# Opening of a two-layer mixer trunk: c and x loaded first, scale and shift rows divided between VectorE and TensorE, rotary tables made inside the group loop

## The chip, the cores and the metric

One core of one Trainium2 chip runs the whole program. The metric is the device time of one execution in microseconds (us), the median of several runs. TensorE (PE) does matmuls and transposes, VectorE (DVE) and ScalarE (ACT) the elementwise work, SyncE (SP) issues every DMA. The program's text is a list of calls; a scheduler gives each engine a fixed order ahead of time, and each engine then runs its own list strictly in that order, held only by semaphores.

## The reference

The kernel computes a trunk of two layers on 256 tokens of width 2048. What this change touches is the head of each layer:

```python
c_act = jax.nn.silu(c)
cos_r, sin_r = rope_tables(positions, RET_DK)
cos_m, sin_m = rope_tables(positions, MLA_ROPE)
...
mod = c_act @ w_mod + b_mod
shift, scale, gate = jnp.split(mod, 3, axis=-1)
h = rms_norm(x, g_norm) * (1.0 + scale[:, None, :]) + shift[:, None, :]
proj = h @ w_in
```

`h` then feeds a retention branch and a latent attention branch, which are gated, merged and projected back. The rotary tables depend on `positions` alone, so they are the same in both layers.

## The kernel before, in words

**Layout.** Activations are kept with features on the partitions: `xT` is 16 blocks of 128 features by 256 tokens. A weight tile is 128 x 1024 f32 (512 KB): SP loads it into `wst` (5 buffers), ACT rounds it to a high part and DVE subtracts to get the low part, both into `whl` (`split_into`, L239 to L241; 3 buffers). A product is three matmuls, high x high, high x low and low x high (`chunk`, L267). One such 512 KB tile is called a chunk below: with 128x256 outputs it is 24 matmuls (16 at L273, 8 at L276), with 128x512 outputs 12.

**The first products.** Before anything else can be multiplied, `h` must exist, and `h` needs 4096 values of scale and shift, each a sum over 2048 rows of `w_mod`. So layer 0 works in four groups of four feature blocks (`GROUPS`, L49). `first_products` (L595) runs 14 columns of `w_in` for one group while the scale and shift rows of the next group are formed in the background: `mod_pair` (L404) loads 16 tiles into `ring` (2 buffers) and DVE adds them, weighted by `cact`, into `macc`. `mod_finish` splits the sum into bf16 pieces, 12 small matmuls with a vector of ones add it over the partitions (`mod_sum`, L351), and DVE puts the result into `mods` (L357) and `amul` (L426). Then DVE normalises a pair of blocks (L446), ACT applies scale and shift (L454) and rounds to `h` high, and DVE makes `h` low (L241). Layer 1 has two groups of eight blocks.

**The opening.** Group 0 has nothing to hide behind, so `start` (L508) writes PE, DVE and ACT's order by hand (`manual_schedule`): the tiles of `w_mod` for group 0 are eight for the scale (`ws[1, k]`) and eight for the shift (`ws[0, k]`), each with two of the 16 row blocks `k`. PE forms the scale row from all 16 (L542, with `cact` as weights); DVE forms the shift row from all 16 (L347, L349), which is summed over the partitions by four matmuls (`mod_sum` at L554). `vectors(0)` (L175) loads `b_mod`, norm gains and `c` as 88 rows and turns them with one transpose. x comes in four 512 KB tiles, is squared by ACT, turned by 32 transposes (L532) and copied to `xT` by ACT (L534). The rotary tables (`rotary_tables`, L215: ten DVE operations on 128x512 or 128x256, then four ACT operations) are made once, in the opening, and read by the rope steps later.

```python
for k0 in range(0, KT - nd, nd):
    mod_rows(acc, ws[0, k0], k0, nd)
A.activation(row[0:1, :], pr[0:1, : ng * P], AF.Copy)
mod_sum(0, 16, ng, [row[0:1, :]], ones[0:1, 0:1])
make_amul(0, 0, ng)
mod_rows(acc, ws[0, KT - nd], KT - nd, nd)
for k in range(ng):
    V.tensor_scalar(xh0[:, k, :], xh0[:, k, :], amul[0][:, k : k + 1], None, ALU.mult)
prepared.append(load_split(first[0], 2, 512, early=True))
mod_sum(0, 0, ng, [acc], ones[:, 0:1])
```

Of the kernel before, what the change touches and what calls it, by code (L numbers as in the profile page):

```python
# [108 lines left out]
def trunk(ctx: ExitStack, tc: tile.TileContext, x, c, positions, w_mod, b_mod, g_norm, w_in, g_cq,  # L109
# [63 lines left out]
    vec = [cp.tile([P, 72 if l else 88], F32, name=f"vec{l}") for l in range(DEPTH)]  # L173

    def vectors(l):  # L175
        rows = tp.tile([P, P], F32, name="rows", tag="tmp")
# [7 lines left out]
        ps = aux_tile()
        T.transpose(ps[:, :r0], rows[:r0, :], ident[:r0, :r0])
        V.tensor_copy(vec[l][:, :r0], ps[:, :r0])

    vectors(0)
# [4 lines left out]
    cact = cp.tile([P, KT], F32, name="cact")  # L193
    A.activation(cact, vec[0][:, 72:88], AF.Silu)

    posi = tp.tile([P, S], I32, name="posi", tag="tmp")
    DMA.dma_start(posi, positions.broadcast_to([P, S]))
    pos = dp.tile([P, S], F32, name="pos", tag="dtab")

# [308 lines left out]
    def start():  # L508
# [6 lines left out]
        row, acc = extra[:, : ng * P], extra[:, 512 : 512 + ng * P]  # L515
        xh0, hh = blocks("xh0"), Pairs("h")
        with tc.manual_schedule(engines={ENG.PE, ENG.DVE, ENG.Activation}):
            for q in range(2):
# [2 lines left out]
            rotary = rotary_tables(quarter("angle"))
            next(rotary)
            v = small(2)
            V.tensor_tensor(v, ss[:, 0, :], ss[:, 1, :], ALU.add)
            V.tensor_scalar(v, v, 1.0 / D, EPS, ALU.mult, ALU.add)
            y = rsqrt_small(v, 2)
            for pair in range(KT // 2):
# [12 lines left out]
            for k0 in range(0, KT, nd):  # L540
                for k in range(nd):
                    T.matmul(pr[0:1, : ng * P], cact[:, k0 + k : k0 + k + 1], ws[1, k0][:, k, :], start=k0 + k == 0,  # L542
                             stop=k0 + k == KT - 1)
            for k0 in range(0, KT - nd, nd):
# [3 lines left out]
            make_amul(0, 0, ng)
            mod_rows(acc, ws[0, KT - nd], KT - nd, nd)
            for k in range(ng):  # L550
                V.tensor_scalar(xh0[:, k, :], xh0[:, k, :], amul[0][:, k : k + 1], None, ALU.mult)
# [479 lines left out]
```

## Time and profile before

| | |
|---|---|
| median of 3 runs | 2054.24 us (2052.72 to 2056.39) |
| the profiled execution's own time | 2055.65 us |
| its span in the trace | 2053.9 us |
| PE busy | 2024.4 us (99%) |
| PE weight loads (PEld) busy | 1807.5 us (88%) |
| DVE busy | 1483.3 us (72%) |
| ACT busy | 1061.9 us (52%) |
| HBM traffic | 223 GB/s over the span |

The span is cut into what each engine did. [...] A row of the timeline gives the start in us, the busy time in us, the engine, the source line, output and inputs, how many instructions, and in brackets how long the engine sat idle before it and what ended that. SPq is SP's queue of DMA issues.

### The profile page before, as it was taken

To read this page: it belongs to the slowest core of one execution; us is meant where nothing else is said; L and a number is where in the kernel's file an instruction comes from. 1 tells how busy PE (TensorE), PEld (TensorE's weight loads), DVE (VectorE), ACT (ScalarE), POOL (GpSimd) and SP (SyncE) were. 2 spreads that over 40 slices of the span, in tenths; PEclk is the share of its full clock that TensorE was granted. 3 is DMA by queue.
4 is the path that set the end of the run, shared out by engine and by line. 5 is a ranking of instruction groups with operands and counts; after the bars stand their busy time and mean duration, and the time that the engine had idled before them with its cause. 6 is when DMAs were issued, how large, how long until landed. Compare 5 with 4: busy or idle time off the path is not lost.

```text
span 2053.9 us, 31775 instructions
## 1 busy us (share of the span) xinstructions
PE 2024.4 (99%) x12412; PEld 1807.5 (88%) x12414; DVE 1483.3 (72%) x2082; ACT 1061.9 (52%) x1489; POOL 0.2 (0%) x4
## 2 busy tenths in 40 slices
PE   7999999999999999999999999999999999999998
PEld 4888898998899998889998888889889999988887
DVE  5789996788777777775577775568766877765574
ACT  4554355644456664444454464456544666644453
POOL 0000000000000000000000000000000000000000
PEclk9999999999999999999999999999999999999999
DMA  8988966567866668875569976665677666666672
GB/s 309 336 287 281 310 202 194 156 191 257 309 191 196 194 185 274 284 267 185 183 197 339 317 214 187 194 180 158 196 240 223 203 186 195 210 224 192 190 243 90
DMA packets 251222, 460.59 MB, mean 224 GB/s; under 512 B 18464, under 2 KB 68032, under 8 KB 251072
## 3 DMA queue, kind: packets, MB, share of 16 engines
q1 hardware_dynamic: 251072, 458.57, 69.9%
q8 instruction: 97, 1.59, 0.3%
q14 instruction: 53, 0.43, 0.1%
HBM read 456.41 MB, written 2.10 MB: 223 GB/s over the span
## 4 chain that ended last, share of the span: by engine, by line
PE 96%; DVE 1%; DMA 1%; ACT 1%; issue 0%; SPq 0%; ACTq 0%; DVEq 0%
PE acc L273 58%; PE acc L276 29%; DMA wmod<-in_w_mod 1%; PE aux L264 1%; PE aux L265 1%; PE aux L263 1%; PE acc L263 1%; PE acc L264 1%; PE acc L265 1%; DVE extra L349 0%; PE aux L882 0%; PE aux L723 0%; PE aux L909 0%; PE aux L848 0%; PE aux L849 0%
## 5 line engine op out<-in xcount | busy, mean ns | idle before, releaser
L240 ACT ACTIVATE whl<-wst 128x1024 fp32r<-128x1024 f32 (+1 forms) x708 | 709.1, 1007 | 810.8 <-PE acc L276 703.4
L241 DVE TENSOR_TENSOR whl<-wst,whl 128x1024 fp32r<-128x1024 f32 (+1 forms) x708 | 814.5, 1156 | 386.7 <-ACT whl L240 383.4
L273 PE MATMUL acc<-whl,h 128*128 128x512 f32 x2048 | 512.2, 391 | 0.0
L273 PEld LDWEIGHTS acc<-whl,h 128*128 128x128 f32 x2048 | 382.1, 188 | 78.2
L273 PE MATMUL acc<-h,whl 128*128 128x256 f32 x2432 | 328.6, 286 | 4.0 <-ACT h L240 2.4
L273 PEld LDWEIGHTS acc<-h,whl 128*128 128x128 f32 x2432 | 308.9, 193 | 6.2 <-ACT h L240 3.2
L276 PE MATMUL acc<-whl,h 128*128 128x512 f32 x1024 | 278.5, 391 | 0.0
L273 PE MATMUL acc<-whl,z 128*128 128x512 f32 x1024 | 254.1, 390 | 1.2 <-ACT whl L240 1.2
L273 PEld LDWEIGHTS acc<-whl,z 128*128 128x128 f32 x1024 | 191.9, 188 | 41.3 <-ACT whl L240 1.6
L276 PEld LDWEIGHTS acc<-whl,h 128*128 128x128 f32 x1024 | 191.3, 188 | 39.5 <-DVE whl L241 0.4
L276 PE MATMUL acc<-h,whl 128*128 128x256 f32 x1216 | 177.8, 286 | 0.0
L276 PEld LDWEIGHTS acc<-h,whl 128*128 128x128 f32 x1216 | 160.2, 194 | 0.0
L276 PE MATMUL acc<-whl,z 128*128 128x512 f32 x512 | 137.3, 389 | 0.0
L402 DVE SCALAR_TENSOR_TENSOR macc<-ring,cact,macc 128x1024 f32<-128x1024 f32 x75 | 96.1, 1281 | 32.0 <-DMA ring<-in_w_mod 31.8
L402 DVE SCALAR_TENSOR_TENSOR macc<-wst,cact,macc 128x1024 f32<-128x1024 f32 x90 | 115.0, 1278 | 0.0
L276 PEld LDWEIGHTS acc<-whl,z 128*128 128x128 f32 x512 | 96.0, 188 | 20.1 <-DVE whl L241 0.2
L273 PE MATMUL acc<-c,whl 128*128 128x256 f32 x640 | 101.1, 289 | 0.0
L273 PEld LDWEIGHTS acc<-c,whl 128*128 128x128 f32 x640 | 86.3, 191 | 0.3
L273 PE MATMUL acc<-m,whl 128*128 128x256 f32 x512 | 67.3, 283 | 0.0
L273 PEld LDWEIGHTS acc<-m,whl 128*128 128x128 f32 x512 | 64.0, 192 | 0.1
L276 PE MATMUL acc<-c,whl 128*128 128x256 f32 x320 | 57.9, 285 | 0.0
L273 PE MATMUL acc<-whl,m 128*128 128x512 f32 (+1 forms) x256 | 56.5, 365 | 0.0
(256 smaller groups left out, 1871.8 us busy)
## 6 DMA issues: line engine op xcount, KB each, us to landing
wst<-in_w_in SPq DMA_DIRECT2D x416, 512.0 KB, 4.4
wst<-in_w_mod SPq DMA_DIRECT2D x96, 512.0 KB, 4.7
ring<-in_w_mod SPq DMA_DIRECT2D x80, 512.0 KB, 5.1
wst<-in_w_ret_proj SPq DMA_DIRECT2D x64, 512.0 KB, 4.8
wst<-in_w_mla_proj SPq DMA_DIRECT2D x64, 512.0 KB, 4.2
wst<-in_w_out SPq DMA_DIRECT2D x64, 512.0 KB, 3.7
wst<-in_w_ukv SPq DMA_DIRECT2D x32, 512.0 KB, 4.3
wst<-in_w_uq SPq DMA_DIRECT2D x32, 384.0 KB, 4.1
```

What stands on the lines that cost most here:

```text
L240: A.activation(hi, src, AF.Copy)
L241: return V.tensor_tensor(lo, src, hi.bitcast(F32), ALU.subtract)
L263: T.matmul(o, a[0], b[0], start=start, stop=False, skip_group_check=True)
L264: T.matmul(o, a[0], b[1], start=False, stop=False, skip_group_check=True)
L265: T.matmul(o, a[1], b[0], start=False, stop=stop, skip_group_check=True)
L273: T.matmul(o, x, y, start=start and i == 0, stop=False, skip_group_check=True)
L276: T.matmul(o, x, y, start=False, stop=stop, skip_group_check=True)
L402: V.scalar_tensor_tensor(macc, w, cact[:, k : k + 1], macc, ALU.mult, ALU.add)
```

## The change

- `c` has a load of its own, directly behind the constants, and is turned and passed through SiLU by itself (PE, then ACT). x is loaded next. `b_mod`, the gains and `positions` are loaded behind the eight scale tiles, and turned and converted after the scale row (`turned()`, and the CAST of `pos`).
- The first four pairs of x blocks are copied to `xT` by DVE, the other four by ACT.
- The scale row is divided: row blocks 0 to 5 on DVE (into `macc`), 6 to 15 on PE (L556 of the new file); eight small matmuls add both parts into one PSUM tile (L563, L566).
- The shift row is divided: row blocks 0 to 11 on DVE, 12 to 15 on PE, with the `w_mod` tile itself as weights and a column of `cact` moving (16 matmuls, L579); four matmuls add DVE's part between them (L583).
- `rotary_tables` is taken out of `start`. It is called in `first_products`, in the loop over the groups and outside the `if` above it, so once for each of the four groups of layer 0 and the two of layer 1. `pos` stays alive until the last of them, in one of the two `dtab` buffers that also hold `r`, the decay tables and the squares of layer 0's end.

```diff
+    crow = tp.tile([P, P], F32, name="crow", tag="tmp")
+    DMA.dma_start(crow[:KT, :], c[0].rearrange("(r q) -> r q", q=P))
...
-        ws = {(i, k): mod_fetch(quarter("wmod"), 0, 16 * i, k, ng) for i in (1, 0) for k in range(0, KT, nd)}
+        ws = {(1, k): mod_fetch(quarter("wmod"), 0, 16, k, ng) for k in range(0, KT, nd)}
+        turned = vectors(0)
+        posi = tp.tile([P, S], I32, name="posi", tag="tmp")
+        DMA.dma_start(posi, positions.broadcast_to([P, S]))
+        ws.update({(0, k): mod_fetch(quarter("wmod"), 0, 0, k, ng) for k in range(0, KT, nd)})
...
+            mod_rows(scale, ws[1, 0], 0, nd)
             for k in range(0, ng, 2):
                 normalise(xh0[:, k : k + 2, :], k, r)
-            next(rotary, None)
+            for k0 in range(nd, on_v, nd):
+                mod_rows(scale, ws[1, k0], k0, nd)
             pr = aux_tile()
...
+            turned()
+            V.tensor_copy(pos[0], posi)
...
+            for k0 in range(0, KT - on_t, nd):
                 mod_rows(acc, ws[0, k0], k0, nd)
...
+            for k0 in range(KT - on_t, KT, nd):
+                for k in range(k0, k0 + nd):
+                    for b in range(ng):
+                        T.matmul(ps[:, b : b + 1], ws[0, k0][:, k - k0, b * P : (b + 1) * P], cact[:, k : k + 1],
+                                 start=k == KT - on_t and b == 0, stop=k == KT - 1, skip_group_check=True)
+                if k0 == KT - on_t:
+                    for b in range(ng):
+                        T.matmul(ps[:, b : b + 1], acc[:, b * P : (b + 1) * P], ones[:, 0:1], start=False, stop=False,
+                                 skip_group_check=True)
+            V.tensor_tensor(mods[0][:, 0:ng], ps[:, :ng], bm[0][:, 0:ng], ALU.add)
             first = [w_in[0, k0 * P : (k0 + 2) * P, n : n + 512] for n in (C_RQ, C_RK) for k0 in range(0, ng, 2)]
             prepared.append(load_split(first[0], 2, 512, early=True))
-            mod_sum(0, 0, ng, [acc], ones[:, 0:1])
...
             if l == 0 and i == 1:
-                vectors(1)
+                vectors(1)()
+            rotary_tables(quarter("angle"), pos[0])
```

Line numbers in the rows below are those of the file they come from; in the changed file the products are L269 and L272, the split L237, `macc` L398, the accumulation L654, `mods` L353, `amul` L422, normalise L442, and `rotary_tables` L216 to L225.

**End of the opening, DVE.** First the kernel before, from the shift row to the first low parts of `h`:

```order
L349 SCALAR_TENSOR_TENSOR extra<-wmod,cact,extra 128x512 x13
L357 TENSOR_TENSOR mod_117<-aux,vec_88 128x4
L426 SCALAR_TENSOR_TENSOR amul_119<-mod_117,vec_88 128x4
L349 SCALAR_TENSOR_TENSOR extra<-wmod,cact,extra 128x512 x2
L551 TENSOR_SCALAR xh_157<-xh_157,amul_119 128x256 x4
L241 TENSOR_TENSOR whl<-wst,whl 128x1024
L357 TENSOR_TENSOR mod_117<-aux,vec_88 128x4
L559 SCALAR_TENSOR_TENSOR h<-xh_157,mod_117,h 128x256 x4
```

Then the change:

```order
L186 COPY vec_88<-aux 128x72
L559 CAST pos<-posi 128x256
L343 TENSOR_SCALAR extra<-wmod,cact 128x512
L345 SCALAR_TENSOR_TENSOR extra<-wmod,cact,extra 128x512 x7
L571 TENSOR_TENSOR mod_106<-aux,vec_88 128x4
L422 SCALAR_TENSOR_TENSOR amul_108<-mod_106,vec_88 128x4
L574 TENSOR_SCALAR xh_153<-xh_153,amul_108 128x256 x4
L345 SCALAR_TENSOR_TENSOR extra<-wmod,cact,extra 128x512 x4
L585 TENSOR_TENSOR mod_106<-aux,vec_88 128x4
L237 TENSOR_TENSOR whl<-wst,whl 128x1024
L216 TENSOR_SCALAR angle<-pos,cst 128x256 x2
L592 SCALAR_TENSOR_TENSOR h<-xh_153,mod_106,h 128x256 x3
```

The copy of `vec`, which needs PE's transpose, now stands ahead of the shift row, the split of the first weight tile has moved behind the addition that makes `mods` (L585), and two table operations stand between it and `h` low.

**End of the opening, PE**, in the change (before, 16 matmuls at L542 and twice four at L356 stand here):

```order
L556 MATMUL aux<-wmod,cact 1x512 x10
L185 MATMUL aux<-cst,rows 128x72
L563 MATMUL aux<-ones,macc 128x1 x4
L566 MATMUL aux<-ones,extra 128x1 x4
L579 MATMUL aux<-cact,wmod 128x1 x8
L583 MATMUL aux<-ones,extra 128x1 x4
L579 MATMUL aux<-cact,wmod 128x1 x8
L269 MATMUL acc<-h,whl 128x256 x16
```

Twelve matmuls (L583 and the second L579) now stand behind DVE's part of the shift row, where four stood.

**From group 1 to group 2 of layer 0, DVE.** First the kernel before:

```order
L446 TENSOR_TENSOR tmp<-xT,r_236 128x512
L357 TENSOR_TENSOR mod_117<-aux,vec_88 128x4 x2
L426 SCALAR_TENSOR_TENSOR amul_119<-mod_117,vec_88 128x4
L446 TENSOR_TENSOR tmp<-xT,r_236 128x512
L241 TENSOR_TENSOR whl<-wst,whl 128x1024
L620 TENSOR_TENSOR rg<-rg,acc 128x512 x2
L241 TENSOR_TENSOR h<-tmp,h 128x512
L241 TENSOR_TENSOR whl<-wst,whl 128x1024
L241 TENSOR_TENSOR h<-tmp,h 128x512
L241 TENSOR_TENSOR whl<-wst,whl 128x1024
L620 TENSOR_TENSOR ma<-ma,acc 128x512 x2
```

Then the change (`ma` is the last column but one and the last of a group):

```order
L353 TENSOR_TENSOR mod_106<-aux,vec_88 128x4
L396 TENSOR_SCALAR macc<-ring,cact 128x1024
L654 TENSOR_TENSOR ma<-ma,acc 128x512 x2
L353 TENSOR_TENSOR mod_106<-aux,vec_88 128x4
L237 TENSOR_TENSOR whl<-wst,whl 128x1024
L398 SCALAR_TENSOR_TENSOR macc<-ring,cact,macc 128x1024
L422 SCALAR_TENSOR_TENSOR amul_108<-mod_106,vec_88 128x4
L398 SCALAR_TENSOR_TENSOR macc<-ring,cact,macc 128x1024
L442 TENSOR_TENSOR tmp<-xT,r_224 128x512
L237 TENSOR_TENSOR h<-tmp,h 128x512
L216 TENSOR_SCALAR angle<-pos,cst 128x256 x2
L237 TENSOR_TENSOR h<-tmp,h 128x512
```

The first `h` of group 2 was made before either `ma` column was added; now it comes behind both. On PE, 61 matmuls of group 1 stood between the second `mod_sum` and group 2's first matmul; now the twelve matmuls of that `mod_sum` are the last thing before it, and none stands between. Between the first `h` low of group 1 and the first of group 2, DVE's list holds 24 splits, 14 `macc` additions, 24 column additions and no table operation before; now it is 29, 16, 28 and 16, and one more `macc` operation that starts a sum.

## Rows read from the trace of the kernel before

**Rows 1.** Page, part 1: busy time and share of the span, by engine.
```profile
PE 2024.4 (99%) x12412; PEld 1807.5 (88%) x12414; DVE 1483.3 (72%) x2082; ACT 1061.9 (52%) x1489; POOL 0.2 (0%) x4
```

**Rows 2.** Windows of 5 us: busy by engine, granted clock, DMA share, GB/s.
```profile
35.00:40.00 5.00, 2.02 (x9) 1.96 (x10) 4.35 (x12) 1.80 (x3) 0.00 (x0) 0.56 1.05 386
...
45.00:50.00 5.00, 5.00 (x40) 5.00 (x40) 1.34 (x2) 2.75 (x4) 0.00 (x0) 0.92 0.71 233
```

**Rows 3.** Timeline of SP's queue, the opening.
```profile
0.73 0.39 SPq L165 DMA_DIRECT2D cst<-in_consts  x1
...
2.80 0.32 SPq L182 DMA_DIRECT2D rows<-in_c  x1
...
3.63 1.93 SPq L205 DMA_DIRECT2D xin<-in_x  x4
```

**Rows 4.** Timeline of DVE, the opening.
```profile
7.22 0.61 DVE L219 TENSOR_SCALAR angle<-pos,cst 128x256 f32<-128x256 f32 x2
...
8.80 3.60 DVE L223 SCALAR_TENSOR_TENSOR angle<-angle 128x512 f32<-128x512 f32 x5
...
24.40 0.49 DVE L347 TENSOR_SCALAR extra<-wmod,cact 128x512 f32<-128x512 f32 x1 [3.35 <-DMA wmod<-in_w_mod]
...
25.84 9.41 DVE L349 SCALAR_TENSOR_TENSOR extra<-wmod,cact,extra 128x512 f32<-128x512 f32 x12 [0.16 <-DMA wmod<-in_w_mod]
...
36.88 1.14 DVE L551 TENSOR_SCALAR xh<-xh,amul 128x256 f32<-128x256 f32 x4
...
39.07 0.15 DVE L357 TENSOR_TENSOR mod<-aux,vec 128x4 f32<-128x4 f32 x1
39.80 1.69 DVE L559 SCALAR_TENSOR_TENSOR h<-xh,mod,h 128x256 fp32r<-128x256 f32 x4 [0.58 <-ACT h L558]
```

**Rows 5.** Timeline of PE, the opening, and eight transposes from later.
```profile
15.29 3.52 PE L532 MATMUL aux<-cst,xin 128*128 128x128 f32 x16 [2.33 <-ACT xT L534]
18.65 0.61 PE L334 MATMUL aux<-tmp,ones 128*128 128x128 f32 x4
19.19 13.89 PE L542 MATMUL aux<-wmod,cact 128*1 128x512 f32 x32
...
37.12 1.83 PE L356 MATMUL aux<-ones,extra 128*128 128x1 f32 x8 [2.31 <-DVE extra L349]
39.82 3.88 PE L273 MATMUL acc<-h,whl 128*128 128x256 f32 x16 [0.87 <-ACT h L558]
...
48.35 2.08 PE L273 MATMUL acc<-h,whl 128*128 128x256 f32 x16
...
495.05 1.06 PE L723 MATMUL aux<-cst,rv 128*128 128x128 f32 x8
```

**Rows 6.** Timeline around group 1's start, PE and DVE.
```profile
122.61 0.51 PE L273 MATMUL acc<-h,whl 128*128 128x256 f32 x2 [1.45 <-ACT h L240]
...
122.59 0.69 DVE L241 TENSOR_TENSOR h<-tmp,h 128x512 fp32r<-128x512 f32 x1 [0.55 <-ACT h L240]
```

**Rows 7.** Window of group 1's first chunks, columns as in rows 2.
```profile
122.60:133.30 10.70, 10.47 (x72) 10.26 (x73) 7.67 (x9) 4.03 (x5) 0.00 (x0) 0.84 0.76 241
```

**Rows 8.** Timeline around group 2's start, PE and ACT.
```profile
188.74 0.45 PE L356 MATMUL aux<-ones_h,part 128*128 128x1 bf16 x12
...
202.99 2.08 PE L273 MATMUL acc<-h,whl 128*128 128x256 f32 x16
...
192.55 0.61 ACT L240 ACTIVATE h<-tmp 128x512 fp32r<-128x512 f32 x1
```

**Rows 9.** Groups by line, DVE, 122.5 to 193.4 us: busy, mean ns, idle before.
```profile
L241 DVE TENSOR_TENSOR whl<-wst,whl 128x1024 fp32r<-128x1024 f32 x24 | 29.1, 1220 | 4.1 <-ACT whl L240 4.0
L402 DVE SCALAR_TENSOR_TENSOR macc<-ring,cact,macc 128x1024 f32<-128x1024 f32 x14 | 17.9, 1280 | 1.0 <-DMA ring<-in_w_mod 1.0
```

**Rows 10.** Timeline of DVE at layer 1's second group, and SP's second decay table.
```profile
1205.68 1.90 DVE L241 TENSOR_TENSOR h<-tmp,h 128x512 fp32r<-128x512 f32 x3 [1.32 <-ACT h L240]
...
362.92 0.35 SPq L736 DMA_DIRECT2D dtab<-in_decay  x1
```

More of the change, by code (lines that the diff above doesn't have):

```diff
@@ L170, in trunk, with turned @@
     V.memset(ones_h, 1.0)
-    vec = [cp.tile([P, 72 if l else 88], F32, name=f"vec{l}") for l in range(DEPTH)]
+    vec = [cp.tile([P, 72], F32, name=f"vec{l}") for l in range(DEPTH)]
     def vectors(l):
         rows = tp.tile([P, P], F32, name="rows", tag="tmp")
-        put = [(b_mod[l], 48), (g_norm[l], 16), (g_cq[l], 4), (g_ckv[l], 4)]
-        if l == 0:
-            put.append((c[0], 16))
         r0 = 0
-        for src, n in put:
+        for src, n in ((b_mod[l], 48), (g_norm[l], 16), (g_cq[l], 4), (g_ckv[l], 4)):
             DMA.dma_start(rows[r0 : r0 + n, :], src.rearrange("(r q) -> r q", q=P))
             r0 += n
[L184 to L188, printed above, removed]
+        def turned():
+            ps = aux_tile()
+            T.transpose(ps[:, :r0], rows[:r0, :], ident[:r0, :r0])
+            V.tensor_copy(vec[l][:, :r0], ps[:, :r0])
+        return turned
+    crow = tp.tile([P, P], F32, name="crow", tag="tmp")
+    DMA.dma_start(crow[:KT, :], c[0].rearrange("(r q) -> r q", q=P))
+    cact = cp.tile([P, KT], F32, name="cact")
     bm = [v[:, 0:48] for v in vec]
@@ L192, in trunk @@
     gckv = [v[:, 68:72] for v in vec]
[L193 to L198, printed above, removed]
     xT = cp.tile([P, KT, S], F32, name="xT")
@@ L205, in trunk @@
             DMA.dma_start(xin[t][q], x[0, t * P : (t + 1) * P, q * 1024 : (q + 1) * 1024])
+    pos = []
     halfpi = cp.tile([P, 1], F32, name="halfpi")
@@ L224, in rotary_tables @@
         V.tensor_scalar(a, a, float(np.pi), float(-np.pi), ALU.min, ALU.max)
-        yield
         A.activation(k, a, AF.Abs)
@@ L511, in start @@
         nd = 8 // ng
-        ws = {(i, k): mod_fetch(quarter("wmod"), 0, 16 * i, k, ng) for i in (1, 0) for k in range(0, KT, nd)}
+        ws = {(1, k): mod_fetch(quarter("wmod"), 0, 16, k, ng) for k in range(0, KT, nd)}
[3 more added lines that the diff above has]
+        ws.update({(0, k): mod_fetch(quarter("wmod"), 0, 0, k, ng) for k in range(0, KT, nd)})
         ss = small(4).rearrange("p (q t) -> p q t", q=2)
         extra, room = quarter("extra"), quarter("room")
-        row, acc = extra[:, : ng * P], extra[:, 512 : 512 + ng * P]
+        row, acc, scale = extra[:, : ng * P], extra[:, 512 : 512 + ng * P], macc[:, : ng * P]
         xh0, hh = blocks("xh0"), Pairs("h")
+        pos.append(dp.tile([P, S], F32, name="pos", tag="dtab"))
+        on_v, on_t = 6, 4
         with tc.manual_schedule(engines={ENG.PE, ENG.DVE, ENG.Activation}):
+            ps = aux_tile()
+            T.transpose(ps[:, :KT], crow[:KT, :], ident[:KT, :KT])
+            A.activation(cact, ps[:, :KT], AF.Silu)
             for q in range(2):
@@ L520, in start, with turn_x @@
                     A.activation(room, xin[t][q], AF.Square, accum_out=ss[:, q, t : t + 1])
[L521 to L527, printed above, removed]
+            def turn_x(pair):
                 ps = aux_tile()
@@ L533, in start @@
                                     xin[t][f // 1024][:, f % 1024 : f % 1024 + P], ident)
-                A.activation(xT[:, 2 * pair : 2 * pair + 2, :].rearrange("p a b -> p (a b)"), ps, AF.Copy)
+                dst = xT[:, 2 * pair : 2 * pair + 2, :].rearrange("p a b -> p (a b)")
+                if pair < KT // 4:
+                    V.tensor_copy(dst, ps)
+                else:
+                    A.activation(dst, ps, AF.Copy)
+            for pair in range(KT // 4):
+                turn_x(pair)
@@ L535, in start @@
+            v = small(2)
+            V.tensor_tensor(v, ss[:, 0, :], ss[:, 1, :], ALU.add)
+            V.tensor_scalar(v, v, 1.0 / D, EPS, ALU.mult, ALU.add)
+            y = rsqrt_small(v, 2)
+            for pair in range(KT // 4, KT // 2):
+                turn_x(pair)
             r = spread(y, dp.tile([P, S], F32, name="r0", tag="dtab"))
+            mod_rows(scale, ws[1, 0], 0, nd)
             for k in range(0, ng, 2):
                 normalise(xh0[:, k : k + 2, :], k, r)
-            next(rotary, None)
+            for k0 in range(nd, on_v, nd):
+                mod_rows(scale, ws[1, k0], k0, nd)
@@ L539, in start @@
             pr = aux_tile()
[L540 to L544, printed above, removed]
-                mod_rows(acc, ws[0, k0], k0, nd)
-            A.activation(row[0:1, :], pr[0:1, : ng * P], AF.Copy)
-            mod_sum(0, 16, ng, [row[0:1, :]], ones[0:1, 0:1])
@@ L548, in start @@
[L548 to L551, printed above, removed]
+            for k in range(on_v, KT):
+                T.matmul(pr[0:1, : ng * P], cact[:, k : k + 1], ws[1, k // nd * nd][:, k % nd, :], start=k == on_v,
+                         stop=k == KT - 1)
+            turned()
+            V.tensor_copy(pos[0], posi)
+            A.activation(row[0:1, :], pr[0:1, : ng * P], AF.Copy)
@@ new lines, in start @@
+            ps = aux_tile()
+            for b in range(ng):
+                T.matmul(ps[:, b : b + 1], scale[:, b * P : (b + 1) * P], ones[:, 0:1], start=b == 0, stop=False,
+                         skip_group_check=True)
+            for b in range(ng):
+                T.matmul(ps[:, b : b + 1], row[0:1, b * P : (b + 1) * P], ones[0:1, 0:1], start=False, stop=True,
+                         skip_group_check=True)
+            for k0 in range(0, KT - on_t, nd):
+                mod_rows(acc, ws[0, k0], k0, nd)
+                if k0 + nd == 8:
+                    V.tensor_tensor(mods[0][:, 16 : 16 + ng], ps[:, :ng], bm[0][:, 16 : 16 + ng], ALU.add)
+                    make_amul(0, 0, ng)
+                    for k in range(ng):
+                        V.tensor_scalar(xh0[:, k, :], xh0[:, k, :], amul[0][:, k : k + 1], None, ALU.mult)
```

7 lines of the change are left out of this document (5 added, 2 removed).

## The prediction

> **What bounds the kernel now.** I read the page first. PE is busy for 99% of the span [rows 1], so the end is set by PE, and only two things can move it: how late PE starts its stream of products, and any hole or slow stretch torn into that stream later. The chain of waits and the timelines of the opening then tell why PE starts late. The DMA engines are full there, 386 GB/s at a share above 1 even at 35 to 40 us [rows 2]. DVE waits until 24.40 us for the first shift tile and then adds without a break, twelve row blocks in 9.41 us [rows 4]; four matmuls after it take 1.83 us, and the products begin at 39.82 us [rows 5]. [...] The first 16 matmuls take 3.88 us where the same take 2.08 later [rows 5]. My yardstick for the opening is the start of the third chunk, 48.35 us [rows 5]; from there a chunk lasts 2.88 us, 24 matmuls at 0.12.
>
> Behind the opening PE waits almost nowhere. One hole stands at group 1's start: 1.45 us for `h` [rows 6], and the window from there shows a clock of 0.84, three chunks in 10.70 us instead of 8.64 [rows 7]. At group 2's start there is none: `h` high was ready at 193.2 us, its first matmul came at 202.99 [rows 8].
>
> **The opening, first half.** Five issues leave SP's front (four row loads and the positions); `cst` and `c`, 0.39 and 0.32 us, remain, so x is issued at about 1.5 us instead of 3.63 [rows 3], 2.1 us earlier. The DMA being full from then on, all the scale tiles land 2.1 us earlier. A 512 KB tile takes 1.35 us at 388 GB/s; the 172 KB of rows and positions now in between cost 0.45 us, so the first shift tile lands at 24.40 - 1.65 = 22.75 us. DVE isn't ready for it. It first copies `vec`, behind a transpose that stands behind PE's ten scale matmuls. These need scale tile 3, five tiles ahead of the first shift tile before, 24.40 - 6.75 - 2.1 = 15.55 us, and take 0.868 us each (13.89/16) [rows 5]: 24.2 us. Transpose, copy and conversion, nearest rows 0.3 us each, bring DVE to 25.1 us. The tables' 5.5 us (0.61, 3.60 and three of 0.43) leave DVE's opening, but stood before x's statistics in idle time: nothing. Copying four x pairs on DVE, bounded by ACT's and DVE's other 128x512 operations, 0.6 to 0.7 us, lies beside ACT's squares: nothing.
>
> **The opening, second half.** DVE: 0.5 + 7 x 0.785 for eight row blocks, `mods`, `amul` and the four scalings 1.6, four more row blocks 3.1: 35.8 us. The same work ended at 36.88 + 1.14 = 38.0 before [rows 4], so DVE gains 2.2 us. Then the tail got longer. Twelve matmuls follow instead of four, 24 records in the trace instead of eight. At the lower clock's 1.83/8 = 0.229 us [rows 5] they take 5.5 us, to 41.4; before, `mods` stood at 39.07. Behind that addition DVE still has the first weight split (pitch 1.14, hidden before in front of it) and two table operations (0.61) before the first `h` low, which PE's second matmul needs: 41.4 + 0.15 + 1.14 + 0.61 + 0.48 = 43.8. Two chunks less one matmul at 0.12 us bring the third chunk to 49.4. The clock decides the ends. If it is high throughout, the tail takes 24 x 0.13 = 3.1 us and the third chunk starts at 47.0: **-1.35**. If the products again run slowly for 6 us as from 39.82 to about 45.8, it is 52.1: **+3.7**. Since PE now works through much of 31 to 43.8 us, I take a rise soon after the products begin, 0.4 us lost: 49.85, **+1.5 us**.
>
> **The tables, six times.** One call is ten DVE operations, 5.5 us, and four on ACT, about 2.2 us and one table load; six calls are 33 us of DVE. Group 0's lies in slack, since its products use DVE for one split and about half a `macc` addition per chunk. In group 1, rows of two calls stand in DVE's list at once.
>
> **Group 1's start.** Four `pos` multiplications, 4 x 0.305 = 1.22 us [rows 4], stand before the first `h` low, where DVE idled 0.55 [rows 6]: **+0.7 us** (0 to 1.5).
>
> **Group 2's start.** Between the first `h` low of groups 1 and 2, DVE's list grows by 16 table operations (10.0 us), five splits (5.7), two `macc` additions and a start (3.1) and four column additions (2.4), 21.2 us. The stretch took 70.7 us, 122.59 to 193.29 (0.7 behind rows 8's `h` high), of which 7.0 are idle, half of it waits for ACT [rows 9]. So it needs 84.9 to 91.9 us; PE needs 202.99 - 122.61 = 80.4. DVE arrives 4.5 to 11.5 us late. The chain says the same: the twelve `mod_sum` matmuls now stand directly ahead of group 2. From their end, before, to `h` high done took 193.16 - 189.19 = 4.0 us, with DVE free [rows 8]. Now a split, a `macc` addition and the adds to `mods` and `amul` come first, some 3.4 us, then two ACT scalings and the rounding 1.7, then `h` low 0.6: **5.7 us** of idle PE, where none was. Such a hole lowers the clock; group 1's start, after 1.45 us, lost 10.70 - 8.64 - 0.22 = 1.8 us [rows 7]. I take **+5.7 +1.8 = +7.5 us**; 4.0 if ACT's chain alone counts and the clock holds, 11.5 if DVE's idle time stays.
>
> **What costs nothing.** Layer 1's second group gets 1.07 us of table work ahead of `h` low, where DVE idles 1.32 us [rows 10]; ACT's extra 2.2 us per call lie in its 48% of free time. `pos` holds one `dtab` buffer, so each decay table must wait for the last to be used; the third was already issued so, at 362.92 [rows 10], and is needed a whole head group later. Uncovered, it would cost its landing, 3.3 us by the DMA view.
>
> **Sum.** +1.5 +0.7 +7.5 = **+9.7 us** on the profiled execution's 2055.65, hence 2065.35. That execution lies 1.41 us above the median of the runs, so I predict 2054.24 + 9.7 = **2063.9 us**.
>
> [...] The transposes of x now run with hardly a gap, from 7.4 to about 14 us, and I let them bring the clock up before the ten scale matmuls. In the trace, 16 transposes at 15.29 take 0.22 us each, eight at a known high clock 0.13, and the matmuls right behind those 16 take 0.15 [rows 5]: the clock rose during a stretch of transposes alone, as their spacing tells. [...]
>
> **Rivals.**
> [...]
> 2. *DVE starves PE inside groups 1 and 2.* The splits come too late by DVE's excess, upper end 11.5 instead of 5.7 us: **2069.7 us**. For it: two table calls among nine splits. Against it: three `whl` buffers, with DVE waiting for ACT 4.0 us in the stretch [rows 9].
> [...]
>
> **How the numbers follow.** A measurement of this kernel can tell about 0.2%, 4.1 us, from no change. Forecast 0.63, rival 1 0.15, rival 2 0.12, rival 3 0.06, and 0.04 for a gain of over 4.1 us by an opening that saves more than any row here shows. The forecast's own terms run from -1.35 + 0 + 4.0 to +3.7 + 1.5 + 11.5; of their combinations about a tenth stay within 4.1 us. So: faster 0.04, same 0.15 + 0.06 = 0.21, slower 0.75. The range that leaves out 2 in 10 runs from 2056 (below rival 1) to 2070 (rival 2).
>
> **What would show it.** Right: SP issues x near 1.5 us; DVE's shift row starts near 25 and ends near 36; `mods` near 41; PE's third chunk near 50; a PE wait of 5 to 6 us at group 2's first matmul, with a clock under 1 behind it; the cosine table made six times; no other new wait. Wrong: no PE wait at group 2, or waits spread over the chunks of group 1; an opening that ends before 47 us; scale matmuls slower than 0.87 us each.

## The result, and the profile after

The changed kernel took **2068.4 us** (median of 6 runs, 2066.51 to 2070.69) against 2054.74 us for the kernel before in the same comparisons (6 runs); the ratio is 1.007, interval [1.006, 1.008]: slower by some 14 us. The profiled execution took 2067.42 us with a span of 2065.6 us, 11.8 us more than the profiled one of before. The page's busy times hardly differ from [rows 1]:

```profile
PE 2029.3 (98%) x12441; PEld 1816.3 (88%) x12443; DVE 1507.8 (73%) x2138; ACT 1069.6 (52%) x1506; POOL 0.2 (0%) x4
```

DVE has 24.5 us more of work, PE 5. The 11.8 us are lost in a few places of the first 300 us. The starts of PE's first matmuls at five places, read from the timelines (us), show where:

| start on PE of | before | after | lost up to here |
|---|---|---|---|
| third chunk | 48.35 | 50.59 | +2.24 |
| group 1 | 122.61 | 124.85 | +2.24 |
| group 2 | 202.99 | 211.31 | +8.32 |
| group 3 | 281.35 | 293.13 | +11.78 |
| first rope matmul (L742, now L776) | 306.22 | 318.01 | +11.79 |

Behind that nothing more is lost: PE's waits from 320 us on are the same groups in both traces, 0.1 us apart.

**Opening.** SP, DVE and PE of the changed kernel, rows of the timeline, to be laid beside [rows 3 to 5]:

```profile
1.64 1.84 SPq L202 DMA_DIRECT2D xin<-in_x  x4
...
25.04 0.48 DVE L343 TENSOR_SCALAR extra<-wmod,cact 128x512 f32<-128x512 f32 x1
...
32.39 3.11 DVE L345 SCALAR_TENSOR_TENSOR extra<-wmod,cact,extra 128x512 f32<-128x512 f32 x4
40.87 0.16 DVE L585 TENSOR_TENSOR mod<-aux,vec 128x4 f32<-128x4 f32 x1 [5.37 <-PE aux L579]
40.95 1.23 DVE L237 TENSOR_TENSOR whl<-wst,whl 128x1024 fp32r<-128x1024 f32 x1
...
15.70 8.74 PE L556 MATMUL aux<-wmod,cact 128*1 128x512 f32 x20 [0.38 <-DMA wmod<-in_w_mod]
...
31.44 3.54 PE L579 MATMUL aux<-cact,wmod 128*128 128x1 f32 x16 [4.97 <-DMA wmod<-in_w_mod]
35.55 1.87 PE L583 MATMUL aux<-ones,extra 128*128 128x1 f32 x8 [0.57 <-DVE extra L345]
37.28 3.55 PE L579 MATMUL aux<-cact,wmod 128*128 128x1 f32 x16
41.63 0.79 PE L269 MATMUL acc<-h,whl 128*128 128x256 f32 x2 [0.80 <-ACT h L591]
43.16 3.36 PE L269 MATMUL acc<-h,whl 128*128 128x256 f32 x14 [0.73 <-DVE h L592]
```

DVE ends its share at 35.5 us, 2.5 earlier than before, and then stands idle 5.37 us for PE's tail. The windows (columns as in [rows 2]; the granted clock is a share of full speed) tell the clock:

```profile
30.00:40.00 10.00, 7.99 (x37) 7.93 (x38) 5.29 (x12) 1.06 (x1) 0.00 (x0) 0.50 0.83 318
40.00:45.00 5.00, 3.47 (x14) 3.09 (x15) 4.13 (x10) 3.60 (x6) 0.00 (x0) 0.50 0.32 92
45.00:50.00 5.00, 5.00 (x36) 5.00 (x35) 4.93 (x7) 1.06 (x1) 0.00 (x0) 0.77 0.55 148
```

The clock had fallen while PE waited 4.97 us for the shift tiles (0.68 over 25 to 30 us). From 31.44 to 40.8 PE ran 128x1 matmuls with one gap of 0.57 us, and the clock stayed at 0.50 all the while.

**Group 2's start.** PE, DVE and ACT, rows of the timeline, to be laid beside [rows 8]:

```profile
205.06 0.45 PE L352 MATMUL aux<-ones_h,part 128*128 128x1 bf16 x12
...
211.31 1.22 PE L269 MATMUL acc<-h,whl 128*128 128x256 f32 x4 [5.79 <-ACT h L236]
213.00 3.35 PE L269 MATMUL acc<-h,whl 128*128 128x256 f32 x14 [0.47 <-DVE h L237]
...
205.72 1.28 DVE L654 TENSOR_TENSOR ma<-ma,acc 128x512 f32<-128x512 f32 x2
206.91 0.15 DVE L353 TENSOR_TENSOR mod<-aux,vec 128x4 f32<-128x4 f32 x1
206.99 1.21 DVE L237 TENSOR_TENSOR whl<-wst,whl 128x1024 fp32r<-128x1024 f32 x1
208.12 1.27 DVE L398 SCALAR_TENSOR_TENSOR macc<-ring,cact,macc 128x1024 f32<-128x1024 f32 x1
209.31 0.15 DVE L422 SCALAR_TENSOR_TENSOR amul<-mod,vec 128x4 f32<-128x4 f32 x1
...
209.50 1.09 ACT L450 ACTIVATE tmp<-tmp,mod,amul 128x256 f32<-128x256 f32 x2 [3.19 <-DVE amul L422]
210.62 0.63 ACT L236 ACTIVATE h<-tmp 128x512 fp32r<-128x512 f32 x1
```

The chain reads down: the last `mod_sum`, which ends at 205.51, DVE's two `ma` columns, which still stand ahead in its list until 206.9, its two additions for `mods` and `amul` with a split and a `macc` addition between them, two scalings and a rounding on ACT, and 5.79 us of idle PE where none was. Behind it the products run slowly:

```profile
212.00:216.00 4.00, 3.53 (x17) 3.24 (x17) 3.18 (x8) 1.72 (x3) 0.00 (x0) 0.50 0.67 231
216.00:220.00 4.00, 4.00 (x28) 4.00 (x28) 3.32 (x5) 1.06 (x1) 0.00 (x0) 0.75 0.00 0
```

### The profile page after: what moved, and what is told of

It is laid out like the page before. It is cut to its first block, busy times and chain, and to the rows that moved or that the text cites. A ratio compares the mean times of both kernels' runs of the same rounds, so it can differ in the third digit from the quotient of the medians.

```text
span 2065.6 us, 31912 instructions
## 1 busy us (share of the span) xinstructions
PE 2029.3 (98%) x12441; PEld 1816.3 (88%) x12443; DVE 1507.8 (73%) x2138; ACT 1069.6 (52%) x1506; POOL 0.2 (0%) x4
## 4 chain that ended last, share of the span: by engine, by line
PE 95%; DVE 2%; DMA 1%; ACT 1%; issue 1%; SPq 0%; ACTq 0%; DVEq 0%
PE acc L269 57%; PE acc L272 28%; DMA ring<-in_w_mod 1%; PE aux L260 1%; PE aux L261 1%; PE aux L259 1%; PE acc L259 1%; PE acc L260 1%; PE acc L261 1%; PE aux L916 0%; DMA wmod<-in_w_mod 0%; PE aux L556 0%; DVE extra L345 0%; ACT whl L236 0%; PE aux L757 0%
## 5 line engine op out<-in xcount | busy, mean ns | idle before, releaser
L237 DVE TENSOR_TENSOR whl<-wst,whl 128x1024 fp32r<-128x1024 f32 (+1 forms) x708 | 814.4, 1156 | 370.8 <-ACT whl L236 367.1
L269 PE MATMUL acc<-whl,h 128*128 128x512 f32 x2048 | 512.1, 391 | 0.0
L269 PEld LDWEIGHTS acc<-whl,h 128*128 128x128 f32 x2048 | 382.0, 188 | 78.0
L269 PE MATMUL acc<-h,whl 128*128 128x256 f32 x2432 | 331.3, 287 | 11.1 <-ACT h L236 8.2
L269 PEld LDWEIGHTS acc<-h,whl 128*128 128x128 f32 x2432 | 310.8, 195 | 13.9 <-ACT h L236 9.1
L272 PE MATMUL acc<-whl,h 128*128 128x512 f32 x1024 | 278.0, 391 | 0.1
L269 PE MATMUL acc<-whl,z 128*128 128x512 f32 x1024 | 254.2, 390 | 1.2 <-ACT whl L236 1.2
L269 PEld LDWEIGHTS acc<-whl,z 128*128 128x128 f32 x1024 | 192.0, 188 | 41.3 <-ACT whl L236 1.6
L272 PEld LDWEIGHTS acc<-whl,h 128*128 128x128 f32 x1024 | 191.3, 188 | 39.7 <-DVE whl L237 0.6
L272 PE MATMUL acc<-h,whl 128*128 128x256 f32 x1216 | 177.3, 285 | 0.0
L272 PEld LDWEIGHTS acc<-h,whl 128*128 128x128 f32 x1216 | 160.1, 194 | 0.1
L272 PE MATMUL acc<-whl,z 128*128 128x512 f32 x512 | 137.3, 390 | 0.0
L398 DVE SCALAR_TENSOR_TENSOR macc<-ring,cact,macc 128x1024 f32<-128x1024 f32 x75 | 96.0, 1280 | 27.9 <-DMA ring<-in_w_mod 27.5
L398 DVE SCALAR_TENSOR_TENSOR macc<-wst,cact,macc 128x1024 f32<-128x1024 f32 x90 | 115.0, 1278 | 0.0
L272 PEld LDWEIGHTS acc<-whl,z 128*128 128x128 f32 x512 | 96.0, 188 | 20.1 <-DVE whl L237 0.2
L269 PE MATMUL acc<-c,whl 128*128 128x256 f32 x640 | 101.1, 289 | 0.0
L269 PEld LDWEIGHTS acc<-c,whl 128*128 128x128 f32 x640 | 86.3, 191 | 0.3
L269 PE MATMUL acc<-m,whl 128*128 128x256 f32 x512 | 67.4, 283 | 0.0
L269 PEld LDWEIGHTS acc<-m,whl 128*128 128x128 f32 x512 | 64.0, 192 | 0.1
L272 PE MATMUL acc<-c,whl 128*128 128x256 f32 x320 | 58.0, 286 | 0.0
L269 PE MATMUL acc<-whl,m 128*128 128x512 f32 (+1 forms) x256 | 56.5, 365 | 0.0
```

The source lines that it names most:

```text
L237: return V.tensor_tensor(lo, src, hi.bitcast(F32), ALU.subtract)
L269: T.matmul(o, x, y, start=start and i == 0, stop=False, skip_group_check=True)
L272: T.matmul(o, x, y, start=False, stop=stop, skip_group_check=True)
L398: V.scalar_tensor_tensor(macc, w, cact[:, k : k + 1], macc, ALU.mult, ALU.add)
```

## The experiments

**The theory** as it stood with the result: the opening costs 2.2 us; the six table calls put DVE in arrears in group 1, which costs 6.1 us of idle PE at group 2 and 3.5 more by a low clock. **Rivals**: the hole at group 2 comes from the new opening; or each call costs its sixth; or the slow products wait for operands, not for the clock. Times are medians, with the ratio to runs of the kernel before on the same chip. The starts of the third chunk and the groups are in the table at the end of this section (in before_filled the third chunk is interleaved with the second; 46.78 is the fourth's 49.66 less 2.88).

**1. Tables only.** The kernel before, its own tables kept, and one more call in each group's turn:

```diff
             if l == 0 and i == 1:
                 vectors(1)
+            for _ in rotary_tables(quarter("angle")):
+                pass
```

> The kernel before, with the tables made in its opening as they were and then once more in each group's turn of both layers (six extra calls); its opening keeps its order and its loads. If the tables alone tear the hole at group 2 (my theory): PE waits 5 to 7 us for h at group 2's first product, the products behind it run 3 us slow, and the third chunk starts at 48.35 as before, or up to 0.6 later for two table operations ahead of the first h low; 2062 to 2065 us in all, +8 to +10. If the hole comes from the new opening (work or waits that it shifts into group 1), there is no wait at group 2 here and the time is within 2 us of 2054.7.

2064.47 us, ratio 1.0044 [1.0027, 1.006], +9.7. PE, group 2's first matmuls:

```profile
208.51 1.22 PE L272 MATMUL acc<-h,whl 128*128 128x256 f32 x4 [6.02 <-ACT h L239]
```

The hole is there without the new opening. The third chunk starts at 47.73, 0.6 before the kernel before's, where I had expected the same or later: the products begin as before, at 39.83, and the first 16 matmuls take 3.88 us as before, but the eight behind them, from 43.50, take 1.52 us instead of 1.91, so by these durations the clock came back a little sooner. So the tables are the larger part, and the first rival falls.

**2. Opening only**, or so I thought: the changed kernel with one call, in group 3's turn (`if l == 0 and i == 3:` ahead of the call).

> The changed kernel, with the tables made once, in group 3's turn, where the instructions' order puts them into group 2's list on DVE; what is left of the change is its opening. If the opening costs 2.2 us by itself and the tables the rest: third chunk at 50 to 50.6, no wait at group 2, at most 2 us of wait at group 3 (DVE's list between the h lows of groups 2 and 3 grows by 9.8 us, before it had about that much in hand); 2056 to 2058 us, +2 to +3. If the hole at group 2 stands with one call too, it is not the tables: 2062 us or more.

2060.33 us, 1.0031 [1.002, 1.0042]. No wait at group 2, but one at group 3, longer than the 2 us expected, and the time lies above its range too:

```profile
284.13 4.07 PE L269 MATMUL acc<-h,whl 128*128 128x256 f32 x18 [3.14 <-ACT h L236]
```

One call is enough to tear a hole, where DVE's list is full: this run isn't the opening alone.

**3. Five calls.** The changed kernel without group 2's call (`if (l, i) != (0, 2):`).

> The changed kernel without group 2's call: five calls stay, and DVE's list in group 1 holds one call's operations in place of two's (8 instead of 16 between the h lows of groups 1 and 2; by list 78.4 us of work, 89.6 with both, 67.8 before). PE needs 80.4 us for that stretch. If DVE's arrears in group 1 are the cause: the wait at group 2 falls from 5.8 to 0 to 2 us, and the time to 2058 to 2062 us. If the price goes with the number of calls (a sixth each of 9.5 us): 2066 to 2067 us, wait 5 us or more.

2066.61 us, 1.0059 [1.0044, 1.0074]: a miss for the time. The wait at group 2 is gone, as the theory of arrears has it, and stands one group later:

```profile
206.05 2.08 PE L269 MATMUL acc<-h,whl 128*128 128x256 f32 x16
...
290.21 4.13 PE L269 MATMUL acc<-h,whl 128*128 128x256 f32 x18 [4.26 <-ACT h L236]
```

From group 2 to group 3 PE took 84.16 us instead of 78.36. The windows between the first `h` low of group 2 and of group 3, here and in the changed kernel (the third busy time is DVE's), show why:

```profile
204.30:290.20 85.90, 80.12 (x465) 70.07 (x463) 80.90 (x98) 38.55 (x45) 0.00 (x0) 0.98 0.86 275
...
212.20:288.90 76.70, 76.23 (x436) 66.89 (x436) 71.01 (x87) 35.29 (x42) 0.00 (x0) 0.96 0.78 254
```

Both stretches hold one call. But the changed kernel has 25 splits and 13 `macc` additions there, this run 30 and 15, in part what stood ahead of group 2's `h` low. The kernel before has 77.1 us of DVE work in this stretch, so the 5.5 us of a call do not fit into PE's 78.36. DVE's arrears are only handed on.

**4. The hole filled.** The changed kernel with extra matmuls in the hole:

```diff
+            if l == 0 and m0 == 16 + GROUPS[0][2][0]:
+                hold = aux_tile()
+                for _ in range(20):
+                    T.matmul(hold, ones_h, pieces[2], start=True, stop=True)
```

> The changed kernel with 20 extra matmuls (128x512 bf16, into a tile that nobody reads) right behind the last twelve mod_sum matmuls, so in the hole at group 2. The hole stays as long for the products, 5.8 us from the last useful matmul, and only the clock can differ. If the slow products behind the hole are the lower clock's (my theory): the extra matmuls take about 0.24 us each, the granted clock stays near 1.00 to 220 us, and from group 2's first product to group 3's it takes 78.4 to 79 us instead of 81.8; 2065 us, 3 us under the changed kernel. If the products there are slow for their operands (splits, weights that come late): 81.8 us again and no gain.

2065.63 us, 1.0052 [1.0037, 1.0067], 2.8 under the changed kernel. The extra matmuls and the window behind the hole:

```profile
205.84 4.26 PE L356 MATMUL aux<-part,ones_h 128*128 128x512 bf16 x19
...
215.00:220.00 5.00, 5.00 (x44) 5.00 (x43) 4.83 (x8) 1.50 (x2) 0.00 (x0) 1.00 0.11 38
```

The clock holds at 1.00, though nothing useful was added. Group 2 to group 3 took 79.89 us instead of 81.82, 0.9 more than expected; it would have been 0.75 less, had DVE's second `h` low not come later (1.22 us of wait instead of 0.47). So of the 3.46 us behind the hole 2.7 are the clock's.

**5. Tables in group 0.** The changed kernel with one call, behind the third pair of columns of group 0:

```diff
                 upto[n] = kg + ng
+                if (l, i, n) == (0, 0, 2):
+                    rotary_tables(quarter("angle"), pos[0])
```

> The changed kernel with the tables made once, in group 0's turn behind its third pair of columns; on DVE the lists between the h lows of groups 1, 2 and 3 are then those of the kernel before, operation for operation. If tables cost their time only through DVE's list in groups 1 and 2: no wait at groups 2 and 3, and what is left over the kernel before is the opening, third chunk at 49.5 to 50.6 against 48.35; 2056 to 2057 us, +1 to +2.3. If one call still costs where it stands, a new wait shows in group 0 and the time is 2059 us or more.

2055.5 us, 1.0004 [0.9995, 1.0014]. No wait at groups 2 and 3, and none in group 0: from the third chunk to group 1 PE takes 73.66 us where it took 74.26, and 0.54 of the difference is a shorter wait at group 1. So here the tables cost nothing, and this is the opening alone. Its third chunk starts at 50.91, 2.56 us late, 0.3 beyond what was expected, but the end is only 1.3 us late. The rest came back at group 1:

```profile
124.57 0.50 PE L269 MATMUL acc<-h,whl 128*128 128x256 f32 x2 [0.91 <-ACT h L236]
...
124.00:128.00 4.00, 3.20 (x24) 3.00 (x25) 3.83 (x6) 2.47 (x5) 0.00 (x0) 1.00 1.02 384
```

The wait is 0.91 us where it was 1.45 [rows 6], and the clock stays at 1.00 where it had fallen [rows 7]: third chunk to group 2 takes 152.57 us instead of 154.64. The difference is ACT's order, here and in the kernel before:

```profile
119.88 1.08 ACT L450 ACTIVATE tmp<-tmp,mod,amul 128x256 f32<-128x256 f32 x2
120.96 1.06 ACT L236 ACTIVATE whl<-wst 128x1024 fp32r<-128x1024 f32 x1
121.92 1.08 ACT L450 ACTIVATE tmp<-tmp,mod,amul 128x256 f32<-128x256 f32 x2
123.40 0.60 ACT L651 ACTIVATE ma<-acc 128x512 f32<-128x512 f32 x1 [0.40 <-PE acc L272]
...
118.39 1.06 ACT L240 ACTIVATE whl<-wst 128x1024 fp32r<-128x1024 f32 x1 [1.33 <-PE acc L276]
119.35 2.21 ACT L454 ACTIVATE tmp<-tmp,mod,amul 128x256 f32<-128x256 f32 x4
121.47 0.57 ACT L618 ACTIVATE ma<-acc 128x512 f32<-128x512 f32 x1
```

Here ACT scales one pair of blocks ahead of rounding a weight and one behind it, and is idle 0.40 us before it copies group 0's last column. In the kernel before it idles 1.33 us ahead of that weight and scales both pairs behind it, and so comes later, against PE, to the copy and to rounding `h`. `before_filled` below and tables_only have the same 0.91 with the old opening, so it is no merit of the new one, but of the order that the scheduler happened upon.

**6. The split first.** As 5, with the first weight split issued ahead of the last addition to `mods`, as before.

> As tables_group0, with the first weight split issued ahead of the last addition to mods, as in the kernel before. If my account of the opening's tail holds (the split stands between mods and the first h low): PE's second matmul of the products no longer waits for h low, the third chunk starts 0.7 to 1.3 us earlier than in tables_group0, and so does the end, 2055 to 2056 us. If the split was hidden behind ACT's rounding of h or behind the slow clock: less than 0.3 us.

2054.99 us, 1.0005 [0.9996, 1.0015]. The products start in one piece, and the third chunk at 49.38, 1.5 us earlier. But group 1 starts at 124.69, as late as in 5: 0.9 us went into a wait for a rounded weight in group 0 (at 87.00); where the other 0.75 us went is open. The step is right, its gain was lost behind it.

**7 and 8. The opening's gaps filled**, in the new opening (6 with 33 extra matmuls) and in the old one (the kernel before with 14), both by

```diff
+            hold = aux_tile()
+            def busy(n):
+                for _ in range(n):
+                    T.matmul(hold[:, :P], ones, ones, start=True, stop=True)
```

> As split_first, with 33 extra matmuls (ones by ones, 128x128, into a tile that nobody reads) in PE's gaps of the opening: 22 ahead of the shift row's matmuls, 8 ahead of those behind DVE's part, 3 behind the last. If the opening loses its time to the lower clock: the granted clock stays at 1.00 from 25 to 50 us, the shift row's 16 records take 2.1 instead of 3.54 us, mods at 38.8 instead of 40.9, third chunk at 45.3 to 46; 2051 to 2053 us, 3 to 4.5 under split_first. If the tail waits for DVE and for landings and not for PE: less than 1.5 us of gain.

> The kernel before with 14 such extra matmuls in its opening: 8 behind the scale row's last matmuls, 6 behind the shift row's. If the clock alone slows its first products: they begin near 39.8 as before (DVE's split sets that), run at the clock 1.00, and the third chunk starts at 45.4 to 46 instead of 48.35; 2051.5 to 2053 us. Against opening_filled this tells what the new opening is worth once the clock is held in both: by my sum 0 to 1 us.

2051.97 us, 0.999 [0.998, 0.9999], and 2051.88 us, 0.9989 [0.9979, 0.9998]: both under the kernel before by 0.1%, and alike. Their third chunks start at 46.75 and 46.78. PE's rows and two windows of the first:

```profile
26.87 6.81 PE L572 MATMUL aux<-ones 128*128 128x128 f32 x44
33.51 1.84 PE L586 MATMUL aux<-cact,wmod 128*128 128x1 f32 x16
...
28.00:30.00 2.00, 2.00 (x13) 2.00 (x12) 1.89 (x4) 0.00 (x0) 0.00 (x0) 0.53 1.06 402
35.00:40.00 5.00, 5.00 (x47) 5.00 (x47) 2.31 (x4) 1.06 (x1) 0.00 (x0) 1.00 1.01 362
```

The 16 records of the shift row take 1.84 us instead of 3.54, and the products run at the full clock from the start. Both third chunks came some 1 us later than I wrote. In the first, the clock fell among the 22 extra matmuls themselves, with PE busy throughout (0.81 from 25 to 30 us, of which 0.53 from 28 on), so that they held the row up until 33.51; in the second, the products began at 40.64 instead of 39.8. With the products at the full clock in both (1.00 from 35 to 50 us), the new opening is worth 0.03 us at the third chunk: nothing. By group 1 the new one is 0.81 ahead, since the old one waits 0.45 us for DVE's `part` in group 0 and loses the rest in smaller amounts there; the medians are 0.1 apart the other way.

Not all that the two gain on the kernel before is the opening's. Of the 2.85 us that before_filled is ahead at group 2, 1.57 stand at the third chunk; the rest is group 1's order of experiment 5, with the wait of 0.91 us and the clock at 1.00 behind it (group 1 to group 2 takes 78.92 us, before 80.38).

**9 and 10. The order of the tail.** All 16 matmuls of the shift row ahead of the four that add DVE's part, without (order_only, on 6) and with 22 extra matmuls.

> As split_first, with that order of the shift row's matmuls and no extra ones. At the lower clock the 32 records need 7.1 us from 30.6 on, then the four: mods at 39.6 to 40 instead of 41.07, third chunk 1 to 1.5 us earlier than split_first's 49.38; 2053.5 to 2055 us. If the order matters less than 0.5 us, PE's time and not DVE's end sets the tail.

> As opening_filled, with all 16 of the shift row's matmuls ahead of the four that sum DVE's part, and 22 extra matmuls in place of 33 (18 ahead of the row, 1 and 3 around the four). If the tail behind DVE's last row block is what the opening now ends on: only four matmuls (1.0 us at the high clock) follow DVE, mods at 37.1 to 37.4 instead of 39.86, third chunk at 44 to 44.6 instead of 46.75, and 2049 to 2050.5 us, 2 to 3 under the best so far and 4 to 5 under the kernel before. If the first weights' splits or landings take over: third chunk at 45.5 or later, or the gain is lost inside group 0 as with split_first (2051.5 us or more).

2054.38 us, 0.9999 [0.999, 1.0009], and 2051.85 us, 0.999 [0.9981, 0.9999]. Without extra matmuls the order brought the third chunk forward by 0.56 us, half of what I expected; the row's matmuls began at 32.07 instead of 30.6, when their tile had landed. With them it came at 47.11, 2.5 us later than expected: the clock fell within the row itself.

```profile
31.16 5.34 PE L586 MATMUL aux<-cact,wmod 128*128 128x1 f32 x32 [0.48 <-DVE mod L578]
...
35.00:40.00 5.00, 5.00 (x25) 5.00 (x25) 2.38 (x5) 1.13 (x3) 0.00 (x0) 0.50 0.91 326
```

**11. The extra matmuls spread** between the rows' matmuls.

> As order_and_fill, with the extra matmuls spread: 20 ahead of the shift row, two behind each of its first three rows of four matmuls and one behind the last, 3 behind the sum of DVE's part. In order_and_fill the granted clock fell to 0.5 to 0.8 between 30 and 45 us, with PE busy but on 128x1 matmuls, behind a wait of 0.48 us. If the 128x1 matmuls in a row let the clock fall: here it stays at 1.00 through 30 to 45 us, the sum of DVE's part follows DVE at 36 to 36.9, mods at 38 to 38.2, third chunk at 44.3 to 45 instead of 47.11; 2049 to 2050.5 us, which would be under both kernels by over 0.2% (ratio to before 0.9975 to 0.998). If the clock falls all the same, or group 0 loses the gain again: 2051.5 us or more.

2053.72 us, 0.9997 [0.9988, 1.0006]: a miss. PE had no gap at all from 25 to 45 us, and the clock fell all the same, to 0.74 over 25 to 30 us, among the extra matmuls, and again to 0.76 over 35 to 40 and 0.55 over 40 to 45; third chunk at 48.34. What mixture keeps the clock is not settled.

**12. The changed kernel again.**

> The changed kernel once more, unaltered. Its first runs lie at 2066.5 to 2070.7, and the profiled one (2067.42, +11.8 over the profiled run of before) below the median (+14.2). If the rest is a clock that recovers at different moments behind the holes: the same waits (opening, 1.45 us at group 1, 5.8 at group 2) and a third chunk or a group 2 that differ by 0.5 to 2 us; median 2067 to 2069 us. If some wait comes and goes: another one in this profile.

2068.08 us, 1.0066 [1.0053, 1.0079]; third chunk 50.67, waits of 1.46 and 5.80 us, group 3 at 293.42. Up to group 3 these are the same waits and the same places within 0.3 us; the 0.5 to 2 us of the expectation do not show there. In layer 1 two waits for a low part are new, 0.20 us at 1168.86 and 0.43 at 1175.06. The profiled execution here is at 2068.61, so the first one was a low one of its kind.

| run | median us | third chunk | group 1 | group 2 | group 3 | rope |
|---|---|---|---|---|---|---|
| tables_only | 2064.47 | 47.73 | 121.39 | 208.51 | 290.22 | 315.10 |
| opening_only | 2060.33 | 49.94 | 123.60 | 202.51 | 284.13 | 310.86 |
| five_calls | 2066.61 | 51.39 | 125.64 | 206.05 | 290.21 | 316.89 |
| hole_filled | 2065.63 | 50.78 | 125.04 | 211.56 | 291.45 | 316.33 |
| tables_group0 | 2055.5 | 50.91 | 124.57 | 203.48 | 281.81 | 306.69 |
| split_first | 2054.99 | 49.38 | 124.69 | 203.60 | 281.93 | 306.80 |
| opening_filled | 2051.97 | 46.75 | 120.41 | 199.33 | 277.66 | 302.53 |
| before_filled | 2051.88 | 46.78 | 121.22 | 200.14 | 278.46 | 303.34 |
| order_only | 2054.38 | 48.82 | 123.47 | 202.38 | 280.71 | 305.58 |
| order_and_fill | 2051.85 | 47.11 | 120.77 | 199.68 | 278.01 | 302.88 |
| mixed_fill | 2053.72 | 48.34 | 122.00 | 200.93 | 279.28 | 304.15 |

Opening_filled and order_and_fill beat both kernels, by 0.1% and 0.8%; so does the kernel before with 14 extra matmuls, which is the smallest edit. The 0.1% is at the edge of what these runs can tell.

## Why the prediction was right, and where it was off

Direction, place and mechanism held: +9.7 us were predicted, +11.8 measured between the profiled runs, and the time lies within the range, at its upper end. Its terms, one by one, in us:

| term | predicted | measured |
|---|---|---|
| opening, third chunk | +1.5 | +2.24 |
| group 1's start | +0.7 | 0.0 |
| group 2's start, idle | +5.7 | +6.1 (5.79 of it one wait) |
| the clock behind it | +1.8 | +3.5 (2.7 of it clock) |
| sum | +9.7 | +11.8 |

**Opening, first half.** x issued at 1.64 (1.5), scale matmuls from 15.70 (15.55) at 0.874 us each (0.868), DVE's shift row from 25.04 (25.1) to 35.5 (35.8), `mods` at 40.87 (41.4): each step within 0.6 us. The third rival, by which the ten scale matmuls would begin slowly, fell with it. Only four records of 128x128 matmuls and waits of 0.55 and 0.38 us stand between the transposes and the scale matmuls, and these run at the high clock from their first (589 to 593 ns a record; in the kernel before 591 to 592, with the granted clock at 1.00 from 20 to 35 us); among the transposes themselves a record lasts 421 ns from 9.7 to 12.9 us and 273 ns from 13.3 us on, where the eight at 495.05 in the kernel before have 272 as their median at a granted clock of 1.00. (The granted clock of the windows reads 1.00 in the first and the second us of the trace already, before PE's first matmul at 2.95, so the durations are the evidence here.)

**Opening, second half: the step that failed** is "I take a rise soon after the products begin, 0.4 us lost", with its reason, that PE works through much of 31 to 43.8 us. It worked (7.99 of the 10 us from 30 to 40), but the clock stayed at 0.50 through that work and the first products. No run shows the 0.4 us; in their place the 22 matmuls from 43.16 to 47.72 lost 1.9 us to the clock (4.56 less 22 x 0.12). `h` low, ready for them at 43.16 instead of 43.8, gave 0.6 of that back.

**Group 1's start.** The four table operations did stand ahead of the first `h` low, but PE waits for `h` high from ACT, and that wait stayed 1.45 us; only inside the chunk 0.45 us were waited for a rounded weight, where 0.22 had been for `h` low. A term for work that was beside the path.

**Group 2's start** went as the chain of the prediction had it. From the end of the twelve `mod_sum` matmuls to `amul` done it took 3.95 us (3.4 predicted): 1.4 until DVE was through with the `ma` columns, which the prediction did not count, and 2.55 for the split, the `macc` addition and the two adds. ACT took 1.7 (1.7). The 0.6 for `h` low was not in that wait, since PE's first matmuls need only `h` high; it showed as the 0.47 behind it. The sum came right with one part too small and one misplaced. The check by DVE's list took 7.0 us of idle DVE from rows 9; the window from 122.59 to 193.29 has 64.73 us busy, so 6.0 idle, and the range becomes 5.5 to 11.5 us late, with the 5.7 still inside.

**The clock behind it** was taken over from group 1's hole of 1.45 us: 1.8 us. Behind 5.79 us the products lost 3.5 us, 2.7 of it to the clock by experiment 4 and 0.47 to the wait for `h` low. That is the other mis-sized term, and in the table the larger. The opening's 0.74 too little and group 1's 0.7 too much cancel, which is luck; the 2.1 us that the sum lacks are the 1.7 here and 0.4 of group 2's start.

**The rivals.** The first, that the clock holds and the gap at group 2 is ACT's 4.0 us alone (2057.6 us), failed on both: the clock fell to 0.50, and the gap was 5.79 us. The second failed too, DVE did not starve PE inside the groups: PE's waits from 45 to 200 us are those at group 1's start. What I wrote at nothing stayed at nothing in this profile: layer 1, the decay tables, ACT and the copies of x. (In changed_again layer 1 has the two waits of experiment 12, 0.6 us.) What I did not see is experiment 3's lesson, that without group 2's call the price would have moved to group 3.

By medians it is 13.7 us, 1.9 more than between the profiled executions: before's lies 0.9 above the median of these runs, after's 1.0 below its own. I had taken off the first (as 1.41, against the three runs known then) and could not know the second. So the 2063.9 us that I forecast are 4.5 short of the median: 2.1 by the terms, 2.4 by these two.

## What to carry to other kernels

Work without a consumer nearby is free only on an engine whose list has room before the next thing that the bottleneck waits for: the same ten DVE operations cost nothing in group 0, 3.1 us of wait in group 2's list, and two sets of them 5.8 us in group 1's, although DVE was idle 27% of the whole. Taking such work out of one stage may just hand the lateness to the next, so look at every deadline behind it. And before an opening is re-divided between engines, read the granted clock there: 14 useless matmuls in the old opening brought its third chunk forward by 1.57 us, where the whole new division put it back by 2.24.

## What was not expected of the hardware

- A busy TensorE was not one at the full clock here: through 9.4 us of 128x1 matmuls (31.44 to 40.8 us, one gap of 0.57) the granted clock stayed at 0.50, and in the order_and_fill run it fell to 0.50 within 32 records of that form. In opening_filled, with 16 records of 128x128 matmuls between two stretches of them, it was 0.84 from 30 to 35 us and 1.00 from 35 us on. In mixed_fill, with four records between every eight, it fell, to 0.76 from 35 to 40 and 0.55 from 40 to 45. And it fell among 128x128 matmuls in a row: in opening_filled it was 0.53 from 28 to 30 us and in mixed_fill 0.74 from 25 to 30, with PE busy without a gap, behind 16 records of 128x1 and 1x1 matmuls; in order_and_fill, with the same records ahead, it was 1.00 from 25 to 30. The runs do not tell what makes the difference.
- Behind a wait of 0.91 us and one of 0.2 at group 1's start the clock stayed at 1.00, in eight profiles out of eight; behind 1.45 us and 0.2 to 0.5 it fell, in all five (before: 0.57 in 124 to 128 us; the others: 0.72 to 0.77 in their lowest windows of 4 us), and in tables_only behind 0.91 and 0.96, to 0.71. So half a microsecond of an ACT rounding's lateness costs some 2 us here (154.64 us from the third chunk to group 2 against 152.57).
- An edit that touches neither group moves the scheduler's order at group 1 and with it that half microsecond: differences of 2 us between such kernels are not told apart by the edit's own reasoning, only by reading that place.
